# Hybrid gMLP and SSD layer on one core: plain A operands kept in rounded parts, y's transposes and stores moved

## The chip, the cores and the metric

One Trainium2 chip; the program runs on one of its cores. The metric is device time of one execution in microseconds (us), the median of several runs. Engines are named as in the profile: PE is TensorE's matrix multiply and PEld its weight load, DVE is VectorE, ACT is ScalarE, POOL is GpSimd, and SP is the engine whose queue issues every DMA of this kernel.

## What is computed

One layer of a decoder trunk over 2048 positions of 1024 channels, in float32:

```python
h = rms_norm(x, pre_w)
proj = jnp.einsum('bld,dc->blc', h, w_in)
u, v, zg, z, xbc, dt_raw = jnp.split(proj, SPLITS, axis=-1)
y_a = spatial_gating(u, v, zg, v_norm_w, v_norm_b, ws, bs, gmlp_norm_w)
y_b = ssd_mixer(xbc, z, dt_raw, conv_w, conv_b, dt_bias, a_log, d_skip, ssd_norm_w)
mixed = jnp.einsum('blc,cd->bld', jnp.concatenate([y_a, y_b], axis=-1), w_out)
return x + rms_norm(mixed, post_w)
```

`spatial_gating` is the gMLP branch: 8 heads of 128 channels, a 128x128 causal matrix per head over chunks of 128 positions, times a SiLU gate, RMS-normed. `ssd_mixer` is a Mamba-2 branch: 16 heads in 4 groups, a causal convolution of width 4, a scan over chunks of 128 positions, a SiLU gate and a grouped RMS norm.

## The kernel before

**Units.** The two large products (input and output projection) are cut into seven units (`UNITS`, line 707). Units 0 and 2 make the SSD inputs x, B and C of two groups each, unit 1 makes z, unit 3 makes v, units 4 and 5 make u and zg of the gMLP, and unit 6 is the output projection. Every unit is a 2x2 block product in Winograd's form, with seven block products P1 to P7 in place of eight (`PRODS`). P1, P2 and P4 take a block of the left operand A as it is (`PLAIN_A`, line 44). P6, P7, P5 and P3 take sums and differences of blocks.

**Steps and runs.** A step is one product, one pair of row blocks `p`, and one part `j` of the contraction. There are 28 steps in each of units 0 to 5 and 56 in unit 6 (the list `steps`, lines 818 to 824). A step has four runs, one for each `c`, and a run is two calls of `mm3` (lines 164 to 167). `mm3` multiplies in float32 precision with rounded parts: an operand is split into a high and a low fp32r part, and high x high, high x low and low x high are added in PSUM. So a step is 24 matmuls on tiles named `acc`, at lines 165, 166 and 167, and a unit of 28 steps has 672 of them. A place is written below as step.matmul: 101.4 is before matmul 4 of the 101st block of 24 `acc` matmuls in PE's order, counted from 0. Unit 1 begins at 28.0, unit 2 at 56.0, unit 3 at 84.0, unit 4 at 112.0, unit 5 at 140.0.

**Operands.** `split` (line 157) makes the parts of a 128x1024 tile: ACT rounds it (line 160), and DVE subtracts to get the low part (line 161). `make_a` (line 720) makes A's operand of a step. For P1, P2 and P4 it loads a block of 512 KB from `hd` (the normed input, written in unit 0) into a tile `r` and splits it, in every unit. For the other four products unit 0 forms the sum, splits it and stores both parts (1 MB) to `a_d` (line 776), and units 1 to 5 load the parts straight into a tile `a` (line 732). `a` has 3 buffers and `r` has 7. `look_ahead` (line 829) asks for A two steps ahead and for B three steps ahead.

**Work between the matmuls.** `after` (line 864) takes a finished accumulator out of PSUM on ACT or DVE. After P1 a copy is taken by ACT (`p`, line 872), and P2 goes on adding in the same accumulator, so PE's first matmul of P2 waits for that copy. Accumulators have five PSUM banks (`pj`). Everything else that PE does has three banks (`ps`): the transposes and small products of the SSD, of the gMLP, and the transposes `y_tp` (line 552).

**Streams.** The small work is a set of Python generators (`tasks`) that are advanced between runs. `ssd_stream` (line 474) goes through 16 pairs (row block, group). For each pair it does the start (`tok_x`, `tok_b`, `decay`, `exps`) and then four chunks (`operands`, `chunk`), beside which the next pair's convolution runs, and ends with `norm`, which scales y on ACT (line 471) and makes a generator `out` of its transposes (`y_tiles`, line 546). `spatial` (line 573) and `gate_out` (line 621) are the gMLP's. Its tiles `v`, `y`, `sg` and the SSD's `zs`, `xdt`, `xde`, `y`, `yo` all come from one pool of 22 buffers (`qpool`).

**Stores.** `store` (line 224) puts a store in a list with a due time, `BEHIND` after the present one, and `flush` issues what is due. Time is counted in units in which a run is 1.36 (`RUN`).

The order in which each engine takes its instructions is set when the program is built, by a scheduler that may move instructions past one another.

Of the kernel before, what the change touches and what calls it, by code (L numbers as in the profile page):

```python
# [8 lines left out]
F32 = mybir.dt.float32  # L9
# [18 lines left out]
EPS = 1e-6  # L28
RUN = 1.36
SPACE = 2.5  # L30
BEHIND = 2.7
LOOK_A = 2
LOOK_B = 3

# [17 lines left out]
def hybrid_kernel(ctx: ExitStack, tc: tile.TileContext, x, x_t, pre_w, w_u, w_o, w_dt,  # L52
# [27 lines left out]
    def rt(name):  # L80
# [2 lines left out]

    hd = [[dram.tile([P, 2, T], F32, name=f"hd{b}_{j}") for j in range(4)] for b in range(NB)]
    a_d = [{(m, j): dram.tile([P, 2, 2, T], F32, name=f"as{p}{m}{j}") for m in PRODS for j in range(2)
            if m not in PLAIN_A} for p in range(2)]
    s_d = {(p, m, j): dram.tile([P, 2, T], F32, name=f"s{p}{m}{j}") for p in range(2) for m in ("S2", "S3")
           for j in range(4)}
    t3_d = [dram.tile([P, 2, T], F32, name=f"t3{j}") for j in range(4)]
# [134 lines left out]
    def store(dst, src, then=None):  # L224
        stores.append((now[0] + BEHIND, dst, src, then))

# [247 lines left out]
    def ssd_stream():  # L474
        order = [(b, 2 * u + n) for u in range(2) for n in range(2) for b in range(NB)]

        def ready(b, g):
            return all((bb, g) in raw_in for bb in range(b + 1))

        cur, prev = Ssd(*order[0]), None  # L480
        for i in range(4):
            cur.load_raw(i)
            if i % 2:
                yield 5
                cur.conv(i - 1)
                yield 0
                cur.conv(i)
                yield 0
        cur.silus()
        for n in range(len(order) + 1):  # L490
            nxt = Ssd(*order[n + 1]) if n + 1 < len(order) else None
            if nxt:
                while not ready(nxt.b, nxt.g):
                    yield 5
            if cur:
                while (cur.b, cur.g // 2) not in zs_in:
                    yield 5
                for c in range(NT):
                    cur.load_e(c)
                cur.tok_x(0)  # L500
                yield 0
                cur.tok_x(1)
            if prev:
                next(prev.out, None)
            yield 0
            if cur:
                cur.tok_b()
                cur.decay(0)
                cur.decay(1)
                yield 0  # L510
            if prev:
                next(prev.out, None)
            if not cur:
                return
            if nxt:
                nxt.load_raw(0)
            cur.load_z(0)
            cur.decay(2)
            cur.decay(3)
            yield 0  # L520
            cur.exps()
            cur.load_z(1)
            yield 0
            cur.operands(0)
            yield 0
            for c in range(NT):
                if nxt:
                    nxt.conv(c)
                    if c + 1 < NT:
                        nxt.load_raw(c + 1)  # L530
                yield 0
                if c + 1 < NT:
                    cur.operands(c + 1)
                cur.chunk(c)
                if c + 2 < NT:
                    cur.load_z(c + 2)
                yield 0
            if nxt:
                nxt.silus()
            cur.norm()  # L540
            yield 0
            prev, cur = cur, nxt
# [78 lines left out]
    def gate_out(b, hp):  # L621
        yg, ss = gate[b, hp], g_ss[b, hp]
        r = rsqrt_mean(ss[:, :, :].rearrange("p c i -> p (c i)"), NT * 2, 1.0 / P, "g")
        for c in range(NT):
            for i in range(2):
                nc.scalar.activation(yg[c][:, i * P:(i + 1) * P], yg[c][:, i * P:(i + 1) * P], AF.Copy,  # L626
                                     scale=r[:, 2 * c + i:2 * c + i + 1])
        yield 8
        yield from y_tiles(b, yg, hp)


# [88 lines left out]
    def make_a(u, p, name, j):  # L720

        piece = lambda m, k: a_piece(u, p, m, k, j)
        tt = nc.vector.tensor_tensor
        if name in PLAIN_A:
            t, = load([piece(*PLAIN_A[name])])
            yield
            yield split(apool, "a", t)
            return
        if 0 < u < 6:
            yield  # L730
# [6 lines left out]
        if name == "P6":  # L737
            if u == 0:
# [7 lines left out]
                t = r  # L746
# [248 lines left out]
```

## Time and profile before

| | |
|---|---|
| median of 3 runs | 1606.11 us (1606.04 to 1612.49) |
| the profiled execution | 1609.79 us |
| its span on the core | 1608.0 us |
| PE busy | 1515.3 us, 94% of the span |
| PEld busy | 1259.7 us, 78% |
| DVE busy | 1129.0 us, 70% |
| ACT busy | 870.8 us, 54% |
| POOL busy | 408.7 us, 25% |
| moved by DMA | 456.88 MB, 284 GB/s over the span |

The span runs from the first to the last instruction of the profiled execution; the execution's own time is 1.8 us longer. Matmul ends are modelled in the profile, and a matmul is drawn over the next one, so PE's busy share does not tell how much of the time it works at its full rate. The gaps between starts tell that. Waits are told by the view of waits: engine, tile and line that waited, then whom it waited for, the sum in us, how often, and the longest.

### The profile page before, as it was taken

The page shows a single profiled execution, that of the slowest core. Times are in us where ns is not written, and L with a number is a line of the kernel's source. Part 1 is how long each engine was busy: PE and PEld are TensorE (multiplying, and loading weights), DVE is VectorE, ACT ScalarE, POOL GpSimd, SP SyncE. Part 2 cuts the span into 40 slices and gives each one's busy share as a digit, 9 for nine tenths or more (in the row PEclk, how much of TensorE's full clock was granted, in tenths as well). Part 3 has the DMA queues.
Part 4 walks back from the last instruction along what each step waited for, and adds up shares of the span by engine and source line. Part 5 has one row for each costly group of instructions (what it writes and reads, how often), then busy time and mean ns, then how long its engine had stood idle before and what let it go on. Part 6 is the DMA issues. An engine that isn't in the chain of part 4 may idle for free. (4 is left out here: it accounts for less than half of the span.)

```text
span 1608.0 us, 21653 instructions
## 1 busy us (share of the span) xinstructions
PE 1515.3 (94%) x7268; PEld 1259.7 (78%) x7268; DVE 1129.0 (70%) x1756; ACT 870.8 (54%) x1823; POOL 408.7 (25%) x449
## 2 busy tenths in 40 slices
PE   4979999999989999999899899998999999999996
PEld 4768888778778888778778788787888887888875
DVE  4466876677676687677778669696676645687698
ACT  4431325666576654665466765879647743333332
POOL 1000000323332333342224434364624300000022
PEclk9987999999999999999999999999999999999998
DMA  8699999968788697786787776757866689797998
GB/s 334 251 365 348 334 416 337 343 224 285 273 274 291 222 328 273 255 300 238 259 285 233 251 268 217 260 175 250 293 222 233 216 278 331 259 380 247 336 357 327
DMA packets 159119, 456.88 MB, mean 284 GB/s; under 512 B 18848, under 2 KB 35616, under 8 KB 146720
## 3 DMA queue, kind: packets, MB, share of 16 engines
q1 hardware_dynamic: 159008, 455.51, 80.2%
q8 instruction: 57, 0.93, 0.2%
q14 instruction: 54, 0.44, 0.1%
HBM read 348.35 MB, written 107.09 MB: 283 GB/s over the span
## 5 line engine op out<-in xcount | busy, mean ns | idle before, releaser
L165 PE MATMUL acc<-b,a 128*128 128x512 f32 x1344 | 543.4, 405 | 19.7 <-ACT sg L614 4.9
L167 PE MATMUL acc<-b,a 128*128 128x512 f32 x1344 | 526.4, 396 | 4.6 <-DVE a L161 4.2
L166 PE MATMUL acc<-b,a 128*128 128x512 f32 x1344 | 528.7, 393 | 0.0
L165 PEld LDWEIGHTS acc<-b,a 128*128 128x128 f32 x1344 | 254.4, 189 | 75.0 <-ACT sg L614 5.5
L167 PEld LDWEIGHTS acc<-b,a 128*128 128x128 f32 x1344 | 254.1, 189 | 60.1 <-DVE a L161 5.9
L166 PEld LDWEIGHTS acc<-b,a 128*128 128x128 f32 x1344 | 254.9, 190 | 49.7
L160 ACT ACTIVATE a<-r 128x1024 fp32r<-128x1024 f32 x144 | 151.8, 1056 | 242.1 <-PE acc L167 115.6
L161 DVE TENSOR_TENSOR a<-r,a 128x1024 fp32r<-128x1024 f32 x144 | 179.0, 1244 | 70.1 <-ACT a L160 69.7
L165 PE MATMUL acc<-a,b 128*128 128x512 f32 x448 | 182.5, 415 | 16.6 <-ACT b L160 5.8
L372 DVE SCALAR_TENSOR_TENSOR cv_out<-cv_raw,cw,cv_out 128x512 f32<-128x512 f32 x192 | 161.2, 848 | 36.9 <-ACT cv_out L370 35.5
L166 PE MATMUL acc<-a,b 128*128 128x512 f32 x448 | 180.4, 403 | 0.5 <-DVE a L161 0.5
L167 PE MATMUL acc<-a,b 128*128 128x512 f32 x448 | 179.2, 404 | 0.0
L161 DVE TENSOR_TENSOR b<-r,b 128x1024 fp32r<-128x1024 f32 x112 | 144.2, 1290 | 40.8 <-ACT b L160 40.7
L160 ACT ACTIVATE b<-r 128x1024 fp32r<-128x1024 f32 x112 | 117.3, 1051 | 72.1 <-DVE r L815 17.5
L165 PEld LDWEIGHTS acc<-a,b 128*128 128x128 f32 x448 | 87.1, 195 | 37.1 <-ACT b L160 5.9
L184 ACT ACTIVATE junk<-y 128x128 bf16<-128x128 f32 (+1 forms) x192 | 65.5, 341 | 85.9 <-POOL y L465 72.5
L457 POOL TENSOR_TENSOR state<-state,ex 128x256 f32<-128x256 f32 x60 | 54.4, 906 | 217.6 <-PE y_ps L451 217.3
L166 PEld LDWEIGHTS acc<-a,b 128*128 128x128 f32 x448 | 87.3, 195 | 19.1 <-DVE a L161 1.0
L167 PEld LDWEIGHTS acc<-a,b 128*128 128x128 f32 x448 | 86.6, 193 | 18.8 <-issue 0.2
L436 POOL TENSOR_TENSOR xde<-xtok,dte 128x256 f32<-128x256 f32 x64 | 56.2, 884 | 158.5 <-ACT xtok L408 158.4
L173 POOL TENSOR_TENSOR o_r<-o_ms,mhalf 128x1 f32<-128x1 f32 x16 | 18.8, 1187 | 295.5 <-DVE o_ms L171 285.4
L389 ACT ACTIVATE E<-E,cs 128x128 f32<-128x128 f32 x256 | 79.9, 389 | 23.4 <-DMA E<-scr 23.3
(163 smaller groups left out, 2149.8 us busy)
## 6 DMA issues: line engine op xcount, KB each, us to landing
r<-w_u SPq DMA_DIRECT2D x108, 512.0 KB, 4.9
r<-hd SPq DMA_DIRECT2D x96, 512.0 KB, 5.6
a<-as0P SPq DMA_DIRECT2D x40, 1024.0 KB, 7.2
a<-as1P SPq DMA_DIRECT2D x40, 1024.0 KB, 7.0
r<-yd SPq DMA_DIRECT2D x72, 512.0 KB, 5.2
r<-w_o SPq DMA_DIRECT2D x36, 512.0 KB, 5.2
E<-scr SPq DMA_DIRECT2D x64, 256.0 KB, 6.7
yd<-yT SPq DMA_DIRECT2D x64, 256.0 KB, 3.3
```

The costliest lines, as they stand in the source:

```text
L160: nc.scalar.activation(w[:, :, 0, :], t, AF.Copy)
L161: nc.vector.tensor_tensor(w[:, :, 1, :], t, w[:, :, 0, :], ALU.subtract)
L165: nc.tensor.matmul(dst, lhsT=a_hi, rhs=b_hi, start=first, stop=False, skip_group_check=True)
L166: nc.tensor.matmul(dst, lhsT=a_hi, rhs=b_lo, start=False, stop=False, skip_group_check=True)
L167: return nc.tensor.matmul(dst, lhsT=a_lo, rhs=b_hi, start=False, stop=last, skip_group_check=True)
L173: nc.gpsimd.tensor_tensor(r, ms, mhalf[:, 0:n], ALU.pow)
L184: nc.scalar.activation(junk[:, 0:n], src, AF.Square, accum_out=dst)
L372: nc.vector.scalar_tensor_tensor(cv, raw[:, j:j + T], cw[:, ti, j:j + 1], cv, ALU.mult, ALU.add)
L389: nc.scalar.activation(E[:, h, :], E[:, h, :], AF.Relu, scale=-1.0, bias=dts[self.b]["cs"][:, o + h:o + h + 1])
L436: nc.gpsimd.tensor_tensor(h4(xde[:, :]), xc, hv(d["dte"], g, c), ALU.mult)
L457: nc.gpsimd.tensor_tensor(h4(st[:, :]), h4(st[:, :]), ev(d["ex"], 1, g, c), ALU.mult)
```

## The change

Four edits are made.

1. `make_a` takes the old path for P1, P2 and P4 only outside units 2 to 5. In unit 1 the two parts of each split are also stored to `a_d`, which now has entries for all seven products: 12 stores of 1 MB. In units 2 to 5 these three products load both parts from `a_d` straight into `a`, as the other four do: 12 loads of 1 MB in each of four units, in place of 12 loads of 512 KB with an ACT and a DVE instruction each.
2. `ssd_stream` issues the two `y_tp` groups of a finished pair in the first two chunks of the next pair, and no longer in the next pair's start. The last pair's are issued after a wait of 8.
3. `gate_out` waits 14 in place of 8 between the scaling of the gMLP's y and its transposes.
4. `BEHIND` is 5.4 in place of 2.7, so that a store becomes due four runs after its data, not two.

```diff
-BEHIND = 2.7
+BEHIND = 5.4
...
     a_d = [{(m, j): dram.tile([P, 2, 2, T], F32, name=f"as{p}{m}{j}") for m in PRODS for j in range(2)
-            if m not in PLAIN_A} for p in range(2)]
+            } for p in range(2)]
...
                 cur.tok_x(1)
-            if prev:
-                next(prev.out, None)
             yield 0
             if cur:
                 cur.tok_b()
                 cur.decay(0)
                 cur.decay(1)
                 yield 0
-            if prev:
-                next(prev.out, None)
             if not cur:
+                yield 8
+                for _ in prev.out:
+                    yield 0
                 return
...
                     if c + 1 < NT:
                         nxt.load_raw(c + 1)
+                if prev and c < 2:
+                    next(prev.out, None)
                 yield 0
...
-        yield 8
+        yield 14
         yield from y_tiles(b, yg, hp)
...
-        if name in PLAIN_A:
+        if name in PLAIN_A and not 1 < u < 6:
             t, = load([piece(*PLAIN_A[name])])
             yield
-            yield split(apool, "a", t)
+            w = split(apool, "a", t)
+            if u == 1:
+                store(a_d[p][name, j], w[:, :, :, :].bitcast(F32))
+            yield w
             return
```

Below, lines of the changed kernel are up to 4 higher than those of the kernel before (552 becomes 553, 593 becomes 594, 637 becomes 638, 732 becomes 736, 872 becomes 876).

**First place: ACT in the first steps of unit 2, before the copies `p` after P1.** Before, word for word (`E` is the SSD's decay, `btok` and `yT` are copies out of PSUM, `a` the splits):

```order
L394 ACT_TABLE_LOAD
L394 ACTIVATE E<-E 128x512
L389 ACTIVATE E<-E,cs_1411 128x128 x4
L418 ACTIVATE btok<-bt_tp 128x512
L394 ACTIVATE E<-E 128x512 x2
L160 ACTIVATE a<-r 128x2x512
L394 ACTIVATE E<-E 128x512
L554 ACTIVATE yT<-y_tp,y_c 128x512
L872 ACTIVATE p_3812<-acc 128x512
L872 ACTIVATE p_3827<-acc 128x512
```

and in the changed program at the same copies:

```order
L638 ACTIVATE stage<-u_2753 128x512
L471 ACTIVATE y<-y,s_r 128x256 x4
L408 ACTIVATE xtok<-xt_tp 128x512 x2
L376 ACTIVATE cv_out<-cv_out 128x512
L876 ACTIVATE p_3771<-acc 128x512
L418 ACTIVATE btok<-bt_tp 128x512
L389 ACTIVATE E<-E,cs_1423 128x128 x4
L876 ACTIVATE p_3802<-acc 128x512
L876 ACTIVATE p_3810<-acc 128x512
```

The splits `a` and the copies `yT` are gone from there, and the decay and exponentials stand behind the first copies, where they stood ahead of them.

**Second place: PE at the start of an SSD pair in unit 3 (101.3 to 101.6), the transposes `y_tp`.** Before, each of the four transposes of a group waits for its own scaling on ACT, which stands just ahead of it in time:

```order
L165 MATMUL acc<-b,a 128x512
L552 MATMUL y_tp<-ident,y 128x128
L166 MATMUL acc<-b,a 128x512
L552 MATMUL y_tp<-ident,y 128x128
L167 MATMUL acc<-b,a 128x512
L552 MATMUL y_tp<-ident,y 128x128
L417 MATMUL bt_tp<-ident,cv_out 128x128
L552 MATMUL y_tp<-ident,y 128x128
L417 MATMUL bt_tp<-ident,cv_out 128x128 x3
```

and in the changed program the same group, at 104.6 (96 `acc` matmuls after the pair's last product `st_ps` at 100.6; before it was 46 after, from 99.6 to 101.4):

```order
L166 MATMUL acc<-b,a 128x512
L167 MATMUL acc<-b,a 128x512
L553 MATMUL y_tp<-ident,y 128x128 x4
L165 MATMUL acc<-b,a 128x512
L166 MATMUL acc<-b,a 128x512
```

The group now stands in one piece, 50 matmuls further behind its data.

**Third place: SP and PE in step 142, the third of unit 5, where the gMLP's `v` of the unit's first gate is loaded.** Before, the loads of one such set stand so in SP's queue, and 96 `acc` matmuls lie on PE between the release of their buffers and the first product `s_ps` that reads them (125 for the set ahead of this one, which is the one that the changed program loads in step 142):

```order
L230 DMA t51_147<-r_10135 128x1024
L579 DMA v_9932<-vd1_157 128x256
L579 DMA v_9934<-vd1_157 128x256
L579 DMA v_9936<-vd1_157 128x256
L579 DMA v_9938<-vd1_157 128x256
L153 DMA r_10643<-t50_146 128x1024
```

In the changed program:

```order
L736 DMA a_9673<-as0P21_103 128x2048
L153 DMA r_10821<-w_u 128x1024
L736 DMA a_9757<-as1P10_114 128x2048
L359 DMA cv_raw_9484<-raw3_3_187 128x515
L398 DMA zs_9440<-zs1_165 128x256
L580 DMA v_9464<-vd0_168 128x256
L580 DMA v_9466<-vd0_168 128x256
L580 DMA v_9468<-vd0_168 128x256
L580 DMA v_9470<-vd0_168 128x256
```

and on PE (the first six matmuls read `a_9757`; the last row reads `v_9464` and `v_9466`; the `y_tp` group that releases the buffer of `v_9464` stands just ahead of these rows, with one `y_ps` and one `st_ps` between):

```order
L165 MATMUL acc<-b,a 128x512
L166 MATMUL acc<-b,a 128x512
L167 MATMUL acc<-b,a 128x512
L165 MATMUL acc<-b,a 128x512
L166 MATMUL acc<-b,a 128x512
L167 MATMUL acc<-b,a 128x512
L553 MATMUL y_tp<-ident,y 128x128 x4
L448 MATMUL y_ps<-xdt,E 128x64 x4
L451 MATMUL y_ps<-state_243,cv_out 128x256
L453 MATMUL st_ps<-xde,btok 128x256
L553 MATMUL y_tp<-ident,y 128x128 x4
L594 MATMUL s_ps<-v,wsT 128x128 x4
```

Only these six `acc` matmuls lie between a `v` load's release and its first use. Its load, and the load of `a_9757`, whose buffer is released by the last matmul of step 141 and which is read by the next `acc` matmul, stand one behind the other in SP's queue. In the other 15 sets of `v` loads of the changed program the distance is 66 to 169 matmuls.

## Rows read from the trace of the kernel before

**Rows 1.** Windows by unit 0 to 6: stretch, us, busy by engine, PE's clock, DMA.

```profile
0.00:248.00 248.00, 213.81 (x972) 179.23 (x973) 155.48 (x282) 85.39 (x145) 12.29 (x21) 0.93 0.91 343
248.00:441.50 193.50, 186.96 (x901) 155.42 (x900) 134.64 (x191) 119.95 (x215) 57.05 (x61) 0.99 0.82 289
441.50:642.00 200.50, 195.15 (x956) 161.73 (x955) 141.56 (x207) 118.46 (x227) 63.26 (x76) 0.99 0.82 278
642.00:854.00 212.00, 198.49 (x960) 163.63 (x958) 154.34 (x251) 125.33 (x233) 66.47 (x78) 0.98 0.78 267
854.00:1072.00 218.00, 208.91 (x1085) 175.68 (x1085) 167.72 (x289) 156.41 (x409) 96.42 (x104) 0.99 0.70 237
1072.00:1279.50 207.50, 201.49 (x1046) 169.93 (x1045) 142.35 (x249) 149.35 (x415) 88.46 (x90) 0.99 0.68 236
1279.50:1608.00 328.50, 310.46 (x1361) 254.07 (x1359) 232.87 (x293) 115.93 (x182) 24.77 (x21) 0.98 0.87 314
```

**Rows 2.** PE's waits in units 1 to 3 (248 to 854 us).

```profile
PE acc L165 <- ACT p L872: 6.4, 2, 4.1
PE y_tp L552 <- ACT y L471: 4.5, 1, 4.5
PE acc L165 <- DVE p L892: 3.7, 2, 3.1
PE cb_ps L422 <- ACT xtok L408: 2.4, 1, 2.4
PE y_tp L552 <- ACT yT L554: 2.0, 2, 1.6
PE bt_tp L417 <- ACT xtok L408: 1.8, 1, 1.8
```

**Rows 3.** PE's waits in unit 4 (854 to 1072 us).

```profile
PE acc L165 <- ACT sg L614: 4.5, 1, 4.5
```

**Rows 4.** PE's waits in unit 5 (1072 to 1280 us).

```profile
PE acc L165 <- ACT a L160: 3.1, 1, 3.1
```

**Rows 5.** Timeline of PE, 454 to 460 us: start, duration, instruction, idle before.

```profile
453.66 0.39 PE L165 MATMUL acc<-a,b 128*128 128x512 f32 x1
...
454.79 0.39 PE L167 MATMUL acc<-a,b 128*128 128x512 f32 x1
459.27 0.50 PE L165 MATMUL acc<-a,b 128*128 128x512 f32 x1 [4.09 <-ACT p L872]
```

**Rows 6.** Windows at half clock in units 1 to 4: one of five, and their sum.

```profile
459.70:463.10 3.40, 3.40 (x10) 2.62 (x9) 2.60 (x4) 3.40 (x6) 0.00 (x0) 0.50 0.92 287
...
sum 20.40, PE 18.43 PEld 15.68 DVE 16.57 ACT 17.45 POOL 7.36; mean PE 3.69 PEld 3.14 DVE 3.31 ACT 3.49 POOL 1.47
```

**Rows 7.** Page, costliest groups: the splits of A (count, busy, mean ns).

```profile
L160 ACT ACTIVATE a<-r 128x1024 fp32r<-128x1024 f32 x144 | 151.8, 1056 | 242.1 <-PE acc L167 115.6
L161 DVE TENSOR_TENSOR a<-r,a 128x1024 fp32r<-128x1024 f32 x144 | 179.0, 1244 | 70.1 <-ACT a L160 69.7
```

**Rows 8.** Page, DMA issues: count, KB each, median us to landing.

```profile
r<-hd SPq DMA_DIRECT2D x96, 512.0 KB, 5.6
a<-as0P SPq DMA_DIRECT2D x40, 1024.0 KB, 7.2
```

**Rows 9.** DMA issues in unit 5 (1072 to 1280 us).

```profile
a<-as1P SPq DMA_DIRECT2D x8, 1024.0 KB, 5.3
```

**Rows 10.** Line 579, the loads of v.

```profile
DMA to landing us min/median/max: 2.0/4.8/9.8
```

**Rows 11.** Groups on ACT in unit 5: count, busy us, mean ns.

```profile
L626 ACT ACTIVATE y<-y,g_r 128x128 f32<-128x128 f32 x72 | 22.2, 391 | 9.1 <-POOL g_r L173 9.1
...
L584 ACT ACTIVATE v<-v,v_r 128x256 f32<-128x256 f32 x32 | 14.8, 500 | 7.1 <-DVE v L583 7.1
```

**Rows 12.** Windows at the end of unit 0 and the start of unit 1.

```profile
200.00:240.00 40.00, 40.00 (x186) 33.40 (x185) 30.29 (x46) 10.36 (x10) 0.00 (x0) 1.00 1.03 415
240.00:300.00 60.00, 57.71 (x269) 47.74 (x268) 35.32 (x41) 39.03 (x62) 5.28 (x5) 1.00 0.91 323
```

## The prediction

> **What bounds the kernel now.** I read the windows by unit first. Units 1 to 5 take 193.5, 200.5, 212.0, 218.0 and 207.5 us, and each has the same 672 `acc` matmuls [rows 1]. Then I read the rate. In the timeline five `acc` matmuls start in 453.66 to 454.79 us, that is 0.226 us each [rows 5], so 672 of them need 152 us. The rest of a unit is small matmuls, which the change leaves in number, and gaps. So PE sets the time, and only what makes PE stand still, or lets its clock fall, can be won. Next I read who ends PE's gaps. In units 1 to 3 ACT or DVE does, at single places: the copy of P1 twice, 6.4 us; the transposes of y behind ACT's scaling, 4.5; an accumulator behind DVE, 3.7; and at the start of an SSD pair the three shared PSUM banks, which wait for ACT's copies `xtok` and `yT`, 2.4, 2.0 and 1.8 [rows 2]. Unit 4 adds 4.5 behind the SiLU `sg` [rows 3] and unit 5 3.1 behind a split [rows 4]. ACT and DVE are busy for 59% (ACT in unit 2, 118.46 of 200.50) to 77% of these units (DVE in unit 4, 167.72 of 218.00) [rows 1], so they are late in bursts, not on average. Last I read the clock. In units 1 to 4 there are five stretches at half of full rate (granted 0.50, the 1.2 GHz level), 20.4 us in all, and PE was busy for 18.43 of them [rows 6]. One of them, from 459.70 on [rows 6], follows the wait of 4.09 us that ends at 459.27 [rows 5].
>
> **Plain A in two parts.** It takes 48 splits out of units 2 to 5: 48 x 1.056 = 50.7 us of ACT and 48 x 1.244 = 59.7 us of DVE [rows 7]. That is beside PE's work, and by itself worth nothing; it counts where a burst made PE wait. The order shows this at the first place: the copy after P1 in unit 2 stood behind two splits, a copy `yT` and the exponentials, and now stands ahead of the exponentials. I take all of the 6.4 us, and the 4.5 us of `sg` in unit 4, where the order changes in the same way. Of the 3.7 us behind DVE I take half, 1.8 (between nothing and all), since the accumulation on DVE keeps its place and only the splits around it go.
>
> Here a rule speaks against the change. The rows show that ACT and DVE have time to spare and that PE alone is full. The Trainium skill's page "Perfetto Trace Analysis", section "Identifying the Most-Contended Engine", says to improve the engine with the highest occupancy first. By that rule relieving ACT and DVE saves nothing here, and the time would stay at 1606. By rows 2 and 3 it saves what PE's named waits hold, and I go by the rows; the rule's outcome is the first rival.
>
> **What the loads cost.** Each of the 48 loads moves 1 MB in place of 0.5 MB and lands after 7.2 us at the median instead of 5.6 [rows 8]. It is asked for two steps ahead, and two steps hold 48 matmuls of 0.226, 10.8 us, so PE's own matmuls hide it; with one step of cover, 5.4 us, it would cost 1.8 us each. It takes a buffer of `a` that PE must first release, and whatever stands behind it in SP's queue waits too: loads of B, stores, `v` and E. I take 1 us for all of this (0 to 5). In unit 1 the 12 new stores are 12.6 MB. Eight of them (P1 and P2) fall in the first 60 us, where 323 GB/s x 60 us = 19.4 MB already move. Together with 8.4 MB that is 27.8 MB. Just before, 415 GB/s were moved for 40 us while PE stayed full [rows 12], so 27.8 MB need 67 us. The 7 us too much are the upper end; the lower is 0, and I take 3, since the loads have 3.6 us to spare (10.8 less 7.2).
>
> **y's transposes.** Nothing is added or taken away; two groups per pair move from a pair's start to the chunks of the next pair, 50 `acc` matmuls further back at the second place, which is 11 us. The scaling on ACT is then long done, and 4.5 us go. At the start two users of the three banks fewer remain, so the waits behind `xtok` and `yT`, 2.4 + 2.0 + 1.8, go too: 10.7 us together (bounds 4.5 and 10.7: the banks may be short in the chunks instead).
>
> **Clock.** Of the 18.43 us that PE worked at half rate, half, 9.2, was lost. Most of it followed waits that go. I take 7 (0 to 9.2).
>
> **Later stores, later gMLP transposes.** Stores that come due later let SP wait less for data at the head of its queue. Nothing on PE's path waits for them, so they win nothing here. But tiles are held longer. The gMLP and the SSD share 22 `q` buffers, and a `v` load must wait until one is free. That is the third place: in step 142 a 1 MB load of A is issued only when step 141 is over, and is needed at once, and behind it the `v` loads have only six matmuls, 1.4 us, of cover. The A load lands after 5.3 us [rows 9], and PE has only small groups meanwhile, so 2.6 (half hidden) to 5.3. `v` lands after 4.8 us [rows 10], at about the same time; then ACT still has the eight gate scalings ahead, 8 x 0.391 = 3.1, and four of `v`, 4 x 0.5 = 2.0 [rows 11], less the 1.4 of cover: 0 to 3.7. So 2.6 to 9.0; as the order puts ACT's and SP's work one behind the other I take 8, and 1.7 for one more stretch at half clock of 3.4 us [rows 6]. The 3.1 us of rows 4 stood near this place and go. Net +6.6 (bounds -0.5 and +15, if each queue waits twice).
>
> **The sum.** 6.4 + 4.5 + 1.8 + 10.7 + 7 = 30.4 us go. What is late next behind each is an accumulator copy or a PSUM bank that is nearly as late; I leave 4 us for such waits (0 to 15). Then 30.4 - 4 - 1 - 3 - 6.6 = 15.8. From the profiled execution, 1609.8 (its span of 1608.0 and 1.8 around it), that is 1594.0. The profiled execution stands 3.7 above the median of 1606.1, so I forecast **1590.3 us**. Units 0 and 6 I leave as they are.
>
> **Rivals.**
> *The waits only pass on.* ACT's and DVE's bursts come from one schedule; if PE then waits as long for the next late thing, 3 us are left: 1603. Against it: in units 1 to 3 the waits are single places of up to 4.5 us, not many small ones [rows 2]. Chance 0.12.
> *The transfers bind.* 48 x 0.5 + 12 more MB on top of DMA shares of 0.68 to 0.82 [rows 1]. With 7 us lost in unit 1 and 2 more in each of units 2 to 5, 12 us, less the 3 counted, are given back, up to 1600. For it: unit 1 would move 289 GB/s x 193.5 us + 12.6 = 68.5 MB, 354 GB/s. Against it: 415 GB/s with PE full [rows 12]. Chance 0.06.
> *The pile-up in unit 5 spreads, slower.* If the late `v` makes the gMLP late there, each next gate finds its `v` late too. One such turn costs up to 9.0 us by the step above. Four of them, over the first half of unit 5, are 36 in place of 8: 1618. It decides the sign from 24 us on, three turns. For it: the six matmuls of cover, and one queue for all loads. Against it: all other sets of `v` have 66 matmuls or more, 15 us. Chance 0.10.
>
> **How the numbers follow.** The forecast has 0.72, the rivals 0.12, 0.06 and 0.10. A measurement of this kernel can tell about 0.5%, 8 us, from no change. The forecast's own range is 1574 (all named waits and the clock's 9.2 go, 34.5 us, and 2 us of costs stay) to 1601 (15 us of waits pass on in place of 4); some 0.04 of its chance lies above 1598. So faster by more than 8 us has 0.68; within 8 us 0.22, with the first two rivals; slower 0.10. The range with rivals is 1574 to 1607, which leaves out the slower one and a little at the low end.
>
> **What would show it.** Right: 48 splits fewer on ACT and DVE; no wait of `y_tp` behind y's scaling; no wait of over 3 us behind P1's copy in unit 2 or behind `sg` at the start of unit 4; unit 3 nearer 200 us than 212; unit 5 longer than 207.5, with a gap before its third step that ends with a DMA of `a` or `v`. Wrong: units 2 to 4 as long as before with other names behind PE's waits (first rival); PE waiting for loads of `a` or `b`, and unit 1 longer by over 5 us (second); several gaps behind `s_ps` in unit 5 (third).

## The result, and the profile after

The changed kernel takes 1588.09 us (median of 4 runs, 1584.37 to 1596.16), the kernel before 1607.07 us (4 runs, 1606.04 to 1612.49). The ratio is 0.988, with a 95% interval of 0.984 to 0.993. The forecast was 1590.3 in a range of 1574 to 1607, so 2.2 us off and on the side that had the most chance. The profiled execution took 1586.59 us, with a span of 1584.8 us, 23.2 us less than the span before.

The windows by unit answer to [rows 1] (stretch, its length, then busy us and instruction records of PE, PEld, DVE, ACT and POOL, PE's clock, DMA share, GB/s):

```profile
0.00:243.00 243.00, 213.28 (x973) 178.90 (x974) 155.22 (x282) 86.07 (x146) 16.14 (x21) 0.93 0.93 350
243.00:439.00 196.00, 185.67 (x891) 154.17 (x890) 135.05 (x192) 110.04 (x203) 54.99 (x60) 0.98 0.98 370
439.00:632.00 193.00, 191.28 (x951) 160.09 (x951) 123.24 (x193) 110.38 (x219) 58.34 (x74) 1.00 0.89 316
632.00:830.00 198.00, 194.56 (x959) 162.14 (x958) 141.65 (x241) 104.54 (x216) 62.29 (x78) 0.99 0.88 312
830.00:1034.00 204.00, 201.40 (x1045) 169.73 (x1044) 145.92 (x262) 138.97 (x364) 82.06 (x90) 1.00 0.81 286
1034.00:1256.50 222.50, 211.17 (x1090) 177.17 (x1089) 135.57 (x251) 152.11 (x440) 91.20 (x107) 0.98 0.69 237
1256.50:1584.80 328.30, 310.26 (x1370) 253.94 (x1368) 233.79 (x294) 117.79 (x186) 25.27 (x21) 0.99 0.88 315
```

Unit 1 is 2.5 us longer, unit 2 is 7.5 shorter, unit 3 14.0 shorter, unit 4 14.0 shorter, unit 5 15.0 longer. Units 0 and 6 are 5.0 and 0.2 shorter.

PE's waits of unit 1, then of units 2 and 3 together, answer to [rows 2]:

```profile
PE acc L165 <- DMA a<-as0P: 5.7, 1, 5.7
PE acc L165 <- ACT a L160: 3.5, 2, 2.7
...
PE acc L165 <- DVE p L896: 2.6, 2, 2.4
PE cb_ps L422 <- ACT xtok L408: 1.0, 1, 1.0
```

The waits behind the copy of P1 and behind y's scaling are gone, the banks' waits are down to 1.0. Unit 1 now waits for a load of A. In unit 4 the 4.5 us behind `sg` [rows 3] are gone, and the longest wait that is left is 1.5. Unit 5, which had one wait of 3.1 [rows 4], has these:

```profile
PE y_ps L448 <- DVE xdt L434: 4.3, 1, 4.3
PE acc L165 <- ACT p L876: 2.5, 1, 2.5
PE st_ps L453 <- ACT yT L555: 1.0, 1, 1.0
```

The splits of A and the loads, from the page of after, answer to [rows 7, 8]. In the first two rows the last part is the idle time ahead of them; the others end with KB each and the median us to landing:

```profile
L160 ACT ACTIVATE a<-r 128x1024 fp32r<-128x1024 f32 x96 | 101.2, 1057 | 201.3 <-PE acc L167 88.2
...
L161 DVE TENSOR_TENSOR a<-r,a 128x1024 fp32r<-128x1024 f32 x96 | 117.3, 1223 | 50.8 <-ACT a L160 44.1
...
a<-as0P SPq DMA_DIRECT2D x64, 1024.0 KB, 7.5
...
r<-w_u SPq DMA_DIRECT2D x108, 512.0 KB, 6.5
...
r<-hd SPq DMA_DIRECT2D x48, 512.0 KB, 7.7
```

48 splits are gone, 50.6 us of ACT and 61.7 of DVE. `r<-hd` landed after 5.6 us before [rows 8], but the two medians are of different loads: the ones that went are those of units 2 to 5, which took 4.3, and the 38 of unit 0 took 7.4 before and 7.1 after. The loads of B, the same 108 in both kernels, do take longer: 6.5 us in place of 4.9.

**Where the time went.** Three things in these views add up to most of each unit's difference. The first is the sum of PE's waits. The second is the time lost at half clock: half of PE's busy time in such stretches, 10.7 us in units 1 to 5 before (six stretches, 21.31 us busy) and 7.7 after (four, 15.44). The third is small matmuls that cross from one unit to the next. I price one of these from unit 4 before [rows 1]: 208.91 us busy less 672 x 0.226, over the 413 other records, is 0.14 us.

| unit | length | PE's waits | half clock | records x 0.14 | sum of the three |
|---|---|---|---|---|---|
| 1 | +2.5 | 6.4 to 10.4, +4.0 | +0.2 | 10 fewer, -1.4 | +2.8 |
| 2 and 3 | -21.5 | 18.6 to 5.1, -13.5 | -4.2 | 6 fewer, -0.8 | -18.5 |
| 4 | -14.0 | 9.2 to 2.6, -6.6 | -1.7 | 40 fewer, -5.6 | -13.9 |
| 5 | +15.0 | 5.9 to 11.3, +5.4 | +2.7 | 44 more, +6.2 | +14.3 |

So units 4 and 5 must be read together: the records show about 40 matmuls that PE did in unit 4 and now does in unit 5. Together the two units take 426.5 us, 1 us more than before. What the change wins on balance lies in units 2 and 3.

### The profile page after: what moved, and what is told of

It reads as the page before. It is cut to its first block, busy times and chain, and to the rows that moved or that the text cites. A ratio compares the mean times of both kernels' runs of the same rounds, so it can differ in the third digit from the quotient of the medians.

```text
span 1584.8 us, 21521 instructions
## 1 busy us (share of the span) xinstructions
PE 1507.6 (95%) x7268; PEld 1256.2 (79%) x7268; DVE 1070.5 (68%) x1708; ACT 819.9 (52%) x1769; POOL 390.3 (25%) x449
## 4 chain that ended last, share of the span: by engine, by line
PE 55%; DMA 14%; DVE 11%; ACT 8%; issue 3%; POOL 1%; SPq 1%; DVEq 0%; ACTq 0%; POOLq 0%
PE acc L165 15%; PE acc L167 15%; PE acc L166 15%; DMA E<-scr 3%; PE y_ps L448 3%; DMA r<-yd 3%; DMA r<-w_o 2%; ACT E L389 2%; DMA r<-w_u 2%; DVE b L161 2%; PE y_ps L451 1%; PE st_ps L453 1%; DVE a L161 1%; PE y_tp L553 1%; DVE cv_out L372 1%
## 5 line engine op out<-in xcount | busy, mean ns | idle before, releaser
L160 ACT ACTIVATE a<-r 128x1024 fp32r<-128x1024 f32 x96 | 101.2, 1057 | 201.3 <-PE acc L167 88.2
L372 DVE SCALAR_TENSOR_TENSOR cv_out<-cv_raw,cw,cv_out 128x512 f32<-128x512 f32 x192 | 156.2, 816 | 43.5 <-ACT cv_out L370 41.4
L161 DVE TENSOR_TENSOR b<-r,b 128x1024 fp32r<-128x1024 f32 x112 | 142.3, 1273 | 61.8 <-ACT b L160 61.7
L161 DVE TENSOR_TENSOR a<-r,a 128x1024 fp32r<-128x1024 f32 x96 | 117.3, 1223 | 50.8 <-ACT a L160 44.1
L457 POOL TENSOR_TENSOR state<-state,ex 128x256 f32<-128x256 f32 x60 | 44.3, 738 | 243.3 <-PE y_ps L451 243.2
L436 POOL TENSOR_TENSOR xde<-xtok,dte 128x256 f32<-128x256 f32 x64 | 52.8, 832 | 165.0 <-ACT xtok L408 158.9
```

The source lines that it names most:

```text
L160: nc.scalar.activation(w[:, :, 0, :], t, AF.Copy)
L161: nc.vector.tensor_tensor(w[:, :, 1, :], t, w[:, :, 0, :], ALU.subtract)
L372: nc.vector.scalar_tensor_tensor(cv, raw[:, j:j + T], cw[:, ti, j:j + 1], cv, ALU.mult, ALU.add)
L436: nc.gpsimd.tensor_tensor(h4(xde[:, :]), xc, hv(d["dte"], g, c), ALU.mult)
L457: nc.gpsimd.tensor_tensor(h4(st[:, :]), h4(st[:, :]), ev(d["ex"], 1, g, c), ALU.mult)
```

## The experiments

My theory was the prediction's: each edit takes its own waits away, and the costs are the stores in unit 1 and step 142 in unit 5. The main rival was that one edit carries the gain and the others only move it about. Each ratio is to runs of the kernel before on the same chip. Unit lengths are of the profiled executions, from one first `acc` matmul to the next. A profiled execution can lie some us off its version's median: 7.1 and 7.3 above in `e1_parts` and `e14_q24_u0`, 5.1 below in `e9_q24`.

**The edits one at a time.** `e1_parts` has edit 1 alone:

```diff
-        if name in PLAIN_A:
+        if name in PLAIN_A and not 1 < u < 6:
...
+            if u == 1:
+                store(a_d[p][name, j], w[:, :, :, :].bitcast(F32))
```

> Edit 1 alone: plain A stored in parts in unit 1 and loaded in units 2 to 5; transposes, gMLP wait and stores as before. Theory A (the prediction): the copies after P1, the SiLU in unit 4 and half of DVE's wait go (12.7 us) with a third of the clock's 7, less 4 for stores and loads: about 11 us faster, 1596, unit 1 longer by 3, units 2 to 4 shorter. Theory B (relieving ACT and DVE, which have time to spare, is worth nothing): 1606 to 1610, only unit 1 longer. Theory C (the later stores bring the gain): 1603 to 1608.

Measured: 1593.03 us, ratio 0.990 (0.989 to 0.992). Units 2 and 3 take 393.3 us, 19.2 less than before: nearly all that the full change wins there, with y's transposes where they were. PE's waits there sum to 6.7 us in place of 18.6; the largest are

```profile
PE y_tp L552 <- ACT y L471: 3.3, 4, 1.5
PE y_tp L552 <- ACT yT L554: 1.2, 1, 1.2
```

The transposes of y still wait, but for 3.3 us in place of 4.5, and the waits behind `xtok` are gone there. Unit 1 takes 206.4, 13 more; it waits 8.9 us, in four pieces, for loads of A:

```profile
PE acc L165 <- DMA a<-as0P: 8.9, 4, 4.0
```

Units 4 and 5 together take 422.3, against 425.5 before.

`e2_trans` has edit 2 alone:

```diff
-            if prev:
-                next(prev.out, None)
...
+                if prev and c < 2:
+                    next(prev.out, None)
```

> Edit 2 alone: the SSD's y transposes in the next pair's chunks. Theory A: PE's waits behind y's scaling and behind the copies xtok and yT go (10.7 us) with part of the clock's 7: about 13 us faster, 1594, most of it in unit 3, whose wait for y's scaling goes. Theory B, which gives the whole gain to the transposes: 1588. Theory C: 1603 to 1608.

Measured: 1603.50 us, ratio 0.997 (0.996 to 0.999), a gain of some 4 us. Units 2 and 3 take 404.7, 7.8 less, all of it in unit 3, and units 4 and 5 take 431.6, 6 more. The waits of `y_tp` are gone, but others stay:

```profile
PE acc L165 <- ACT p L873: 5.7, 4, 4.1
PE acc L165 <- DVE p L893: 3.1, 2, 2.1
PE cb_ps L422 <- ACT xtok L408: 2.5, 2, 2.2
```

Its units 4 and 5 show that edit 2 by itself moves the small matmuls (1043 and 1094 records, against 1085 and 1046 [rows 1]):

```profile
840.20:1048.70 208.50, 201.73 (x1043) 169.22 (x1042) 158.62 (x278) 147.04 (x380) 82.18 (x93) 1.00 0.72 244
1048.70:1271.80 223.10, 213.42 (x1094) 178.57 (x1094) 149.45 (x259) 159.13 (x444) 94.45 (x101) 0.97 0.68 227
```

`e3_behind` has edit 4 alone:

```diff
-BEHIND = 2.7
+BEHIND = 5.4
```

> Edit 4 alone: stores due after 5.4 instead of 2.7. Theory A: nothing on PE's path waits for a store, so no difference over 4 us: 1602 to 1610. Theory B: the same. Theory C (SP's queue, held up at its head by stores whose data is late, is what delays loads and with them ACT and DVE): 10 us faster or more, under 1597.

Measured: 1633.12 us, ratio 1.016 (1.014 to 1.018), 25 us slower. That is the largest effect of any single edit, of one that I had costed at nothing. 20.4 us of it lie in unit 5 (228.0 in place of 207.6). PE's waits there, and the stretches at half clock, the sum of three:

```profile
PE acc L165 <- ACT a L160: 6.1, 1, 6.1
PE s_ps L593 <- DVE cbm L424: 4.5, 1, 4.5
PE acc L165 <- ACT sg L614: 3.3, 2, 1.9
```

```profile
sum 20.40, PE 16.97 PEld 13.77 DVE 16.37 ACT 15.52 POOL 8.21; mean PE 5.66 PEld 4.59 DVE 5.46 ACT 5.17 POOL 2.74
```

The waits sum to 15.5 us against 5.9, and PE loses 8.5 at half clock against 1.4. A store on SP is on none of these waits. The longest is behind a split on ACT, the next behind the SSD on DVE. That a later store shifts the streams' work so that it meets the splits is how I read this; it is not shown.

**The edits together.** `e4_noparts` is the full change without edit 1 (edits 2, 3 and 4):

```diff
-        if name in PLAIN_A and not 1 < u < 6:
+        if name in PLAIN_A:
```

> Edits 2, 3 and 4 together, without edit 1. Theory A: 13 us from the transposes less 4 for the late loads of v at step 142, which stay without the late load of A: about 1597, 9 us slower than the full change; unit 1 shorter than in the full change by 3 or more, since the stores of plain A and their wait go. Theory B: 1585 to 1588, as fast as the full change or faster, since edit 1 only costs. Theory C: about 1590.

Measured: 1614.74 us, ratio 1.004 (1.003 to 1.005): slower than before. Unit 5 takes 229.2 there. So putting edit 1 under the other three is worth some 26 us (from 7 above the kernel before to 19 below it), though by itself it is worth 15.

`e10_p_t` has edits 1 and 2:

```diff
-BEHIND = 5.4
+BEHIND = 2.7
...
-        yield 14
+        yield 8
```

> Edits 1 and 2 together, without the gMLP's longer wait and the later stores. If the effects of edits 1 and 2 add up (15 and 4 us measured apart), 1588, and edits 3 and 4 are then worth nothing. If the later stores are what lets edits 1 and 2 work together (rival: with stores due early, unit 1 stays at 206 us as with edit 1 alone, where the full change has 196), unit 1 at 200 us or more and 1595 or more.

Measured: 1593.64 us, ratio 0.990 (0.986 to 0.994), the same as edit 1 alone, within what the runs can tell. Neither theory gave this: the sum of the single effects was 1588, the rival's time 1595 or more. But the rival's sign for unit 1 did come: the unit takes 204.1, near the 206.4 of edit 1 alone. The waits behind `xtok` are back in units 2 and 3, 2.6 us.

`e7_gate8` is the full change without edit 3 (edits 1, 2 and 4):

```diff
-        yield 14
+        yield 8
```

> The full change with the gMLP's wait at 8 instead of 14 (without edit 3). The theory that the longer wait keeps tiles and makes step 142 late: the loads of v have 48 matmuls of cover there in place of 6, the 4.3 us wait for xdt behind v on DVE goes, unit 5 under 215 us in place of 222.5, 1580 to 1584. Rival, that unit 5 is long because the SSD's stream runs later and its work falls into unit 5: unit 5 stays at 220 or more, 1586 to 1590.

Measured: 1592.27 us, ratio 0.990 (0.987 to 0.993), and unit 5 still takes 223.8. That the longer wait of 14 is what makes unit 5 long is therefore not borne out.

This kernel and `e10_p_t` differ in `BEHIND` alone. In time they are the same (1592.27 and 1593.64), but two effects of `BEHIND` stand against each other: with the later stores unit 1 takes 196.2 in place of 204.1, and unit 5 takes 223.8 in place of 216.3. In unit 1 SP waits less at the head of its queue for the copies that it is to store. First `e10_p_t`, then `e7_gate8`:

```profile
SPq L230 <- ACT stage L638: 36.6, 17, 6.2
SPq L230 <- ACT stage L638: 12.4, 15, 2.9
```

PE's waits in the unit sum to 10.7 in place of 14.8, those for loads of A to 6.8 in place of 8.2, and it loses 1.7 at half clock in place of 3.4.

`e5_notrans` is the full change without edit 2 (edits 1, 3 and 4), with the lines of `e2_trans` taken back.

> The full change without edit 2: y's transposes at the next pair's start as before. If edit 2 takes away waits of its own (10.7 us by the prediction, 4 alone in e2): 1592 to 1599, with waits behind y's scaling or the copies xtok and yT back in units 2 to 4. Rival, that edit 1 has freed ACT enough that the old place is as good (edit 2 added nothing to edit 1 in e10): 1585 to 1590.

Measured: 1591.65 us, ratio 0.991 (0.988 to 0.993). Unit 4 takes 209.1 and unit 5 223.9. All five versions with edit 1 as written lie between 1588.1 and 1593.6 with intervals that overlap. So edit 1 is enough for most of the gain, and without it the other three together win nothing (`e4_noparts`). By the times, these runs do not settle whether the other three add 5 us or nothing to it. By the unit lengths, edit 4 does two things: unit 1 takes 195.0 to 196.2 in the three with the later stores and 204.1 and 206.4 in the two without, and units 4 and 5 together 426.5 to 433.0 against 422.3 and 423.4.

**Unit 1's cost.** `e13_u2` stores the parts one unit later, and loads them in units 3 to 5:

```diff
-        if name in PLAIN_A and not 1 < u < 6:
+        if name in PLAIN_A and not 2 < u < 6:
...
-            if u == 1:
+            if u == 2:
```

> The full change, but plain A is split in unit 2 too and stored there, and loaded in units 3 to 5. In unit 1 PE waited 5.7 us for a load of A and 3.5 behind a split, with DMA at 0.98 of its time. If the 12.6 MB of stores are the cause: unit 1 at 190 us or less in place of 196, these waits gone, and unit 2, with less traffic, 195 to 200 in place of 193: 1584 to 1588. Rival (the waits are from the order, not from bandwidth): unit 1 stays within 2 us of 196 and unit 2 gets longer, 1592 or more.

Measured: 1596.32 us, ratio 0.993 (0.991 to 0.995). The windows of units 1 to 3:

```profile
246.00:441.00 195.00, 188.88 (x897) 156.89 (x896) 134.39 (x192) 121.11 (x212) 52.38 (x59) 0.97 0.84 295
441.00:645.00 204.00, 197.27 (x972) 164.45 (x971) 143.98 (x210) 119.54 (x229) 69.40 (x79) 0.99 0.96 349
645.00:848.00 203.00, 196.05 (x957) 163.16 (x956) 142.13 (x244) 106.52 (x216) 60.51 (x78) 0.98 0.86 302
```

The DMA share of unit 1 falls from 0.98 to 0.84 and its wait of 5.7 us for a load of A goes (2.3 are left, for another). The stores are what fills unit 1. But the unit is not at the expected 190 or less: it takes 193.9 in place of 196.1. PE's waits fall from 10.3 to 6.0, and half clock takes back 2.4 (a stretch of 10.2 us from 413.0 on). And unit 2 keeps its splits: from first `acc` to first `acc` it takes 200.3 in place of 193.0, unit 3 203.0 in place of 198.0. That loses more than unit 1 gives back.

`e14_q24_u0` goes the other way, with the stores in unit 0 and 24 `q` buffers:

```diff
-    qpool = ctx.enter_context(tc.tile_pool(name="qpool", bufs=22))
+    qpool = ctx.enter_context(tc.tile_pool(name="qpool", bufs=24))
...
-        if name in PLAIN_A and not 1 < u < 6:
+        if name in PLAIN_A and not 0 < u < 6:
...
-            if u == 1:
+            if u == 0:
```

> The full change with 24 buffers, plain A's parts stored in unit 0 already and loaded from unit 1 on. 12 splits fewer in unit 1, and the 12.6 MB of stores in unit 0, where DMA was at 0.91 of its time and PE waited for none of it after the first 120 us. If unit 1's waits for the load of A come from stores and loads that meet there: unit 1 at 190 us or less, unit 0 longer by under 5: 1573 to 1581. Rival (bandwidth is used up in unit 0 too): unit 0 longer by 10 or more and 1585 or more.

Measured: 1614.82 us, ratio 1.005 (1.002 to 1.007). Unit 0 takes 237.6 in place of 206.6 (`e9_q24`, below, which differs only in where the parts are stored), and unit 1 is no shorter for it, 196.2 against 195.1. The two halves of unit 0:

```profile
36.00:156.00 120.00, 96.42 (x437) 79.37 (x438) 63.02 (x109) 40.31 (x73) 4.81 (x6) 0.80 0.98 375
156.00:274.00 118.00, 104.57 (x471) 85.49 (x469) 89.76 (x150) 29.52 (x35) 2.38 (x4) 0.97 1.01 392
```

Here the transfers do bind: a share of 0.98 to 1.01 for all of the unit, and PE's waits of 14.9 us for DVE's `h` and 8.2 for splits of A are for work that reads fresh loads. The longest single wait stands at the unit's end, before the first `acc` of unit 1, and is for a load itself:

```profile
PE acc L165 <- DMA a<-as0P: 11.7, 1, 11.7
```

With it PE's waits in unit 0 sum to 41.0 us against 13.4 in `e9_q24`, and half clock costs 4.0 more: together 31.6, as much as the unit grew. Unit 0 has the stores of the other four products too, and 12 more do not fit.

**Step 142.** `e9_q24` is the full change with two more `q` buffers (22 to 24, the first two lines of the diff above), so that `v` can be asked for earlier.

> The full change with 24 in place of 22 buffers for the small token tiles. If step 142 is late because no such buffer is free for v: v has 39 matmuls of cover in place of 6, the waits in step 142 (7.6 us, of them 4.3 behind DVE) fall to under 3 and the half-clock stretch there goes; unit 5 under 215, 1577 to 1583. Rival (the gMLP's stream is late in itself, buffers or not): the waits stay at 7 or more, 1586 to 1590.

Measured: 1582.15 us, ratio 0.983 (0.979 to 0.986). Unit 5 takes 213.2 in place of 222.6 and unit 4 207.4 in place of 204.1, together 6.1 less than in the full change. At the place of step 142, PE's timeline in the full change (start, duration, what, idle before) is

```profile
1048.04 0.39 PE L167 MATMUL acc<-b,a 128*128 128x512 f32 x1
...
1055.33 0.67 PE L453 MATMUL st_ps<-xde,btok 128*128 128x256 f32 x2 [0.95 <-ACT yT L555]
1055.65 0.58 PE L165 MATMUL acc<-b,a 128*128 128x512 f32 x1
...
1057.22 0.60 PE L553 MATMUL y_tp<-ident,y 128*128 128x128 f32 x4
1062.14 1.97 PE L448 MATMUL y_ps<-xdt,E 128*128 128x64 f32 x8 [4.31 <-DVE xdt L434]
...
1067.35 1.29 PE L594 MATMUL s_ps<-v,wsT 128*128 128x128 f32 x8
...
1068.83 0.49 PE L165 MATMUL acc<-b,a 128*128 128x512 f32 x1
```

and with 24 buffers

```profile
1048.73 0.39 PE L167 MATMUL acc<-b,a 128*128 128x512 f32 x1
1048.96 1.00 PE L448 MATMUL y_ps<-xdt,E 128*128 128x64 f32 x8
1051.44 0.67 PE L453 MATMUL st_ps<-xde,btok 128*128 128x256 f32 x2 [1.48 <-DVE yo L463]
...
1055.91 1.13 PE L594 MATMUL s_ps<-v,wsT 128*128 128x128 f32 x8 [2.43 <-DVE yo L463]
...
1057.24 0.48 PE L165 MATMUL acc<-b,a 128*128 128x512 f32 x1
```

In the full change 20.8 us pass from the last `acc` of step 141 to the seventh of step 142, with only six `acc` between them; with 24 buffers the same place has one pause of 8.5 us. The waits there sum to 4.1 us in place of 7.6. That is not the expected 3 or less, but the pile falls apart, and the half-clock stretch of 6.8 us that the full change has from 1061.0 on is not there.

`e16_before_q24` is the kernel before with 24 buffers and nothing else.

> The kernel before with 24 in place of 22 buffers for the small token tiles. If the shortage is what the change itself brings (v has 95 matmuls of cover or more there with either number): 1603 to 1610, no gain. Rival, that two more buffers help any version of this kernel by 6 us: 1600 or less.

Measured: 1611.39 us, ratio 1.003 (1.002 to 1.005). Two buffers more do not help the kernel before. What `e9_q24` wins is therefore what the change had made scarce, unless it is the new order alone (see Open).

`e18_q24_gate8` has 24 buffers and edits 1, 2 and 4, with the wait of 8.

> The full change with 24 buffers and the gMLP's wait back at 8. v has 90 matmuls of cover or more in every set. If cover for v and free buffers are what unit 5 lacks, it is as fast as e9 or faster, 1574 to 1583, unit 5 at 213 or less. Rival (the wait of 14 does something of its own that is useful): 1586 or more.

Measured: 1582.36 us, ratio 0.985 (0.983 to 0.987), the same as `e9_q24`. With buffers to spare, edit 3 makes no difference. These two are the fastest versions that were run: some 25 us faster than before by medians, and some 6 faster than the full change, though on other chips than its own runs, and their intervals and the full change's just overlap. The second pair with 22 and 24 buffers, `e7_gate8` and this one, says the same: 1592.27 to 1582.36.

## Why the prediction was right, and where it was not

**Right: what bounds the kernel, and where the gain lies.** The forecast took PE as the bound and its named waits as all that can be won. Units 2 and 3 lost 21.5 us, of which 13.5 are waits and 4.2 clock. Unit 3 takes 198, nearer 200 than 212, as it should; there is no wait of `y_tp` behind y's scaling, none of 3 us behind P1's copy, and `sg` at unit 4's start is gone. The first rival, by which the waits only pass on, gave 1603 and falls: PE's waits in units 1 to 5 went from 40.1 us to 29.4. PE was at 94% and ACT and DVE at 54% and 70%, and relieving ACT and DVE alone brought 15 us (`e1_parts`). With it falls what the prediction made of a rule. The Trainium skill's page "Perfetto Trace Analysis", section "Identifying the Most-Contended Engine", says to optimize the engine with the highest occupancy first. That nothing is won by relieving other engines was my inference from it: to end PE's gaps is work on PE, whichever engine the work is taken from.

**Wrong in the sharing out: the terms were not separate.** I gave the splits 12.7 us (6.4, 4.5 and 1.8) and the transposes 10.7, and added them. Measured, the transposes bring 4 us alone and nothing on top of edit 1 that the runs can tell, and the splits bring 15 alone. Moving the transposes does end their own waits (`e2_trans`), but not the banks' waits for `xtok`, which I had put into the 10.7: in units 1 to 3 they sum to 4.7 us where they had been 4.2. Other waits grow in place of those that go, so that PE's waits in units 2 and 3 fall only from 18.6 to 16.0. With edit 1 alone `xtok` is no wait of PE's in units 1 to 3, and y's wait is shorter too (`e1_parts`); with both edits 2.6 us of `xtok` are back (`e10_p_t`). Both edits work on waits behind one late engine, ACT, and part of what they win can be won only once. The step that failed is that the waits behind `xtok` and `yT` "go too: 10.7 us together". The sum came out near because the splits brought more than I gave them, and in part by luck: the errors in unit 1, in unit 5, in the clock and in the later stores went both ways.

**Wrong: "they win nothing here", of the later stores.** In sum that was right beside edits 1 and 2, but as a step it failed: nothing on PE's path waits for a store, yet loads of A stand behind the stores in SP's queue, and PE waits for those (in unit 1 8.2 us with the early stores and 6.8 with the later ones). That explains a part: unit 1 is 8 us shorter with the later stores, and unit 5 some 7.5 longer (`e10_p_t` and `e7_gate8`). I had looked for their cost only in tiles held longer and in step 142. Alone they cost 25 us, 20.4 of them in unit 5, at other places (`e3_behind`); that this is because the splits still stood there to be met is not shown. The third rival, a pile-up in unit 5 that makes the change slower, thus had the right unit and the right sign for two versions that were run, `e3_behind` and `e4_noparts`, though no wait of PE's there is for `v`. In the full change unit 5 grew too, by 15 us; what kept the sign is the 21.5 us that units 2 and 3 won.

**Unit 1: the term was too small, for want of cover.** I took 3 us for the stores and 1 for the loads, from a landing time of 7.2 us and 10.8 us of cover. Around 290 us the DMA engines were busy all the time (a share of 1.02 from 285 to 300 us) and the loads landed after 9.6 and 11.2 us. The view is of the loads of A between 285 and 300 us in the changed kernel:

```profile
DMA to landing us min/median/max: 9.6/10.4/11.2
```

The one that PE waited 5.7 us for is this:

```profile
288.20 0.32 SPq L736 DMA_DIRECT2D a<-as0P  x1
```

It landed after 11.2 us, at 299.4, and PE would have taken it at 293.7. So its cover was 5.5 us; with the 10.8 of the forecast, the long landing would have cost 0.4. It was issued late because SP's queue stood still. In none of the 14 traces is a DMA issued before the eighth one ahead of it has landed, and all six issues from 283.5 to 290.9 us begin within 0.1 us of such a landing (this one at 288.20, after a load of `E` that was issued at 280.96 and landed at 288.14). Long landings thus cost twice: the data is late, and the next issue is. The other loads of A in the unit had more room: their cover was 12.9 us at the median (13.1 before), their landing 9.2 (7.9 before).

Unit 1's waits went from 6.4 us to 10.4, although the wait behind P1's copy (2.3) and the bank's (1.8) went: 8 us of new waits, for this load, for splits and for DVE, where I had 4 for the loads and stores of all units. With edit 1 alone the unit grew by 13 us. The second rival was right about what PE waits for in this unit, and wrong about its length in the full change (2.5 us more, not over 5) and about the other units: units 2 to 4 move 286 to 316 GB/s, and no wait for a load stands in their lists.

**Unit 5: right place, right size, wrong cause.** I took 8 us for step 142 and 1.7 for a stretch at half clock. Measured: the waits around step 142 sum to 7.6 us, and a stretch of 6.8 us begins in the longest of them. But the load of A landed 6.5 us after its issue at 1048.46, ahead of the six `acc` that need it (1055.65), and no wait was for it. The `v` loads landed after 4.5 to 5.0 us and were no wait of PE's either. What PE waited for was DVE, which from 1055.92 on was never idle and did the work in this order:

```profile
1055.92 1.54 DVE L372 SCALAR_TENSOR_TENSOR cv_out<-cv_raw,cw,cv_out 128x512 f32<-128x512 f32 x2 [1.95 <-ACT cv_out L370]
1057.38 0.41 DVE L458 TENSOR_TENSOR state<-state,st_ps 128x256 f32<-128x256 f32 x1
1057.71 0.89 DVE L372 SCALAR_TENSOR_TENSOR cv_out<-cv_raw,cw,cv_out 128x512 f32<-128x512 f32 x1
1058.52 1.81 DVE L584 SCALAR_TENSOR_TENSOR v<-v,v_mv,row_w 128x256 f32<-128x256 f32 x2
1060.26 1.09 DVE L372 SCALAR_TENSOR_TENSOR cv_out<-cv_raw,cw,cv_out 128x512 f32<-128x512 f32 x1
1061.28 0.47 DVE L584 SCALAR_TENSOR_TENSOR v<-v,v_mv,row_w 128x256 f32<-128x256 f32 x1
1061.67 0.41 DVE L434 TENSOR_TENSOR xdt<-xtok,dt 128x256 f32<-128x256 f32 x1
```

`xdt`, which PE needed, stood behind the convolution (3.3 us from 1055.92 on) and three pieces of `v` (2.1). And the convolution itself was late, as the first row shows, by ACT: it had stood idle for 4.19 us until 1052.17, for POOL, and then did the eight gate scalings that the prediction counted, 2.45 us. So the cost came through the order of the work on ACT and DVE, not through the transfer. That the short cover of `v` is behind it is not shown: in `e7_gate8`, built to give `v` 48 matmuls of cover there, the waits at this place still sum to 4.9 us, the stretch of 6.8 us at half clock stays, and unit 5 is as long. Two more buffers ease it (`e9_q24`), so buffers seem scarce there; through which tile is not shown. The rest of unit 5's 15 us I had not seen at all: some 6 us are work that moves over from unit 4, which is no loss. Edit 2 moves it by itself (`e2_trans`), and edits 3 and 4 move as much without it: in `e5_notrans` the two units have 1033 and 1098 records.

**Clock.** I took 7 us of the half-clock time as won, less 1.7 in unit 5, 5.3 net. It was 10.7 less 7.7, 3.0, since stretches also follow the waits that are new in units 1 and 5 or left in unit 3.

**The rest.** Unit 0, which I left as it was, is 4.5 us shorter from first `acc` to first `acc`. The eleven other kernels without plain A's stores in unit 0 have 206.6 to 210.2 there, ten of them under 209, against 210.9 in the profiled execution of before; even `e16_before_q24`, with none of the edits, has 207.6. So I take it for that execution and not for the change, in keeping with the 3.7 us by which it stood above its median.

**Open.** Why stores that are due two runs later cost so much by themselves: no store reads a `q` tile, so it is not the 22 buffers directly. Edit 3 was not tried without edit 4. Whether edits 2 to 4 together add anything to edit 1 is below what these runs can tell. And every edit lets the scheduler set a new order on all engines, so that a part of each difference may be that order and not the mechanism named; the kernel before got 4 us slower from two buffers more (`e16_before_q24`). No run holds the order fixed.

## What to carry to other kernels

When one engine is the bound and two others stand behind each of its gaps, take work out of the others where they are late: their mean load says nothing about it. Do not add up waits that have one late engine in common; two cures for it win once. And when a change of several parts wins, time the parts: here one carried the gain, one cost 25 us alone, and a pool two buffers larger, worth nothing before, was worth some 6 us after. Look at the parts by stage as well: a part that is worth nothing in sum won 8 us in one unit and lost as much in another.

## What the runs showed of the hardware that was not expected

**Landing times rise well before PE starves.** In unit 1 the DMA engines were busy for 0.98 of 196 us and moved 370 GB/s, and PE lost only 5.7 us to a load, the one with the least cover. Over the whole kernel the 512 KB loads of B (`r<-w_u`) went from a median of 4.9 us to 6.5, and from 285 to 300 us, at a share of 1.02, a 1 MB load took 11.2. In `e14_q24_u0` one took 13.0, with 1.4 us of cover, and PE waited 11.7 for it.

**Eight transfers under way, and no more.** In all 14 traces, with 1106 or 1118 DMAs each, SP issues no DMA before the eighth ahead of it has landed, while the seventh ahead was still under way at 237 to 342 of the issues. Their landings are told by eight semaphores in turn; whether the program alone or the chip sets the number, no run here shows. In a full stretch the cover that the program asks for is then cut by the landing times of what was issued before.

**The clock falls after some short gaps and not after others.** In the changed kernel a stretch at 0.50 or 0.51 comes with PE's waits of 2.4 us to 818.1 (it begins at 818.7) and of 2.5 us to 1098.9 (it begins at 1098.5), but none comes with the 2.67 us that end at 256.66. In the 5.7 us wait the clock fell before the wait had ended: the stretch begins at 296.4 and the load came at 299.4.
